# Attention weights kept as running products and met with differences of neighbouring values

## The chip, the cores and the metric

The kernel runs on one core of a Trainium2 chip. The core has five engines with instruction queues of their own, each worked off in order: TensorE (PE, matmuls and transposes; its weight loads are listed as PEld), VectorE (DVE), ScalarE (ACT), GpSimd (POOL) and SyncE (SP, which issues most DMAs here). The metric is the device time of one execution in microseconds (us).

## The reference

One decoder layer on 1,024 tokens and 16 meta tokens, width 1,024, all in float32. An input projection feeds four branches (a gated recurrence, a pooling branch, stick-breaking attention, a short convolution); they are gated, mixed and projected, and a squared-ReLU MLP follows. The change touches the attention branch alone, 8 heads of 64:

```python
def stick_breaking_attention(q, k, v, valid):
    # A[t,s] = sigmoid(z_ts) * prod_{s<j<t} (1 - sigmoid(z_tj)), s < t
    def one_block(args):                      # 128 queries
        ...
        z = jnp.einsum('bqhd,bkhd->bhqk', q_blk, kh) * scale
        log_keep = jnp.where(mask, jax.nn.log_sigmoid(-z), 0.0)
        between = lax.cumsum(log_keep, axis=3, reverse=True) - log_keep
        A = jnp.where(mask, jnp.exp(jax.nn.log_sigmoid(z) + between), 0.0)
        return jnp.einsum('bhqk,bkhd->bqhd', A, vh)
```

## The kernel before

The kernel is written in Python loops that are unrolled; a scheduler then puts each engine's instructions in an order of its own, with the order of the program as priority. What an engine runs is therefore not quite what the code's order says.

Every float32 product is done as two or three matmuls on a high part and a low part (`split`: ACT writes the high part, DVE subtracts it to get the low part). Tokens lie in reverse order of time, so that "earlier" keys have higher columns, and the 16 meta tokens come last, as a ninth block. `L` is 1,040, `P` is 128, `NB` is 8.

The attention works on pairs of heads (`Pair`, four of them): one pair's Q, K and V are 128 rows, 64 a head. A `Step` is one head `e` of the pair and one block `j` of 128 queries, with `n = 1040 - 128 j` keys (1,040, 912, ... 144): 16 steps to a pair, 64 in all. Each step has these parts:

- `scores`: PE makes the scores in chunks of up to 512 columns into the two banks `z`; ACT turns each chunk into `keep` (sigmoid of -z, shifted by a column) and `sig` (sigmoid of z); POOL masks the first 128 columns of both (`affine_select`); DVE forms the running product of `keep` with a scan, and multiplies `sig` by it. The result in `sig` are the attention weights.
- `turn`: PE transposes the weights, 128 columns at a time, into the two banks `tr`; `split` writes them to `at_h` and `at_l`.
- `combine`, once for two steps: PE multiplies `at_h` and `at_l` with the pair's values `vv` into the bank `av`; ACT copies one half to `fold`, DVE adds it to the other half into `br`, the branch's output.
- `values`, once for a pair: PE transposes the pair's V, and `vv` gets its high and low part.

Step i's scores are issued together with step i-1's transposes and, on odd i, with the `combine` of the two steps before. Between these parts stands filler: `fill` yields groups of three projection matmuls (the next pair's Q, K and V, 24 x 3,104 columns; for the last pair the first tile of the convolution branch), and after each part the loop takes up to `FILL` = 1,400 columns of it:

```python
for p in parts:
    if next(p, None) and i < NS:
        owed = spend(owed + FILL)
```

A pair has 65 parts that take filler, and 65 x 1,400 is more than 74,496 columns, so the filler of a pair ends before the pair does. Before the attention stand the norm of the tokens and the first pair's projections, behind it the recurrence, the pooling, the gates, the mixing and the MLP.

Of the kernel before, what the change touches and what calls it, by code (L numbers as in the profile page):

```python
# [10 lines left out]
F32 = mybir.dt.float32  # L11
# [4 lines left out]
ALU = mybir.AluOpType  # L16
# [15 lines left out]
WINDOWS = (2, 4, 8, 16)  # L32
FILL = 1400
QCH = [(0, 512), (512, 512)]
# [10 lines left out]
def hybrid_trunk_kernel(ctx: ExitStack, tc: tile.TileContext, x_tok, metas, vecs, gains, w_in, w_br, w_pool,  # L45
# [156 lines left out]
    with ExitStack() as st:  # L202
        pl = pool("attn", 1, None, st)
        VW = (NB + 1) * P
        sig = [new(pl, [P, VW], F32, f"sig{i}") for i in range(2)]
        keep = [new(pl, [P, (L, LP - 16)[i]], F32, f"keep{i}") for i in range(2)]
        for i in range(2):
            nc.gpsimd.memset(sig[i], 0.0)
            nc.gpsimd.memset(keep[i][:, 0:1], 1.0)
        A, B = slice(0, 64), slice(64, 128)  # L210
# [43 lines left out]
        class Pair:  # L254
            def __init__(self, pr):
                self.pr = pr
                self.qs, self.kh = ([new(pl, [P, w], F32R, tag, 4) for _ in range(2)]
                                    for w, tag in ((T, "qs"), (LP, "kh")))
                self.kl = kls[pr % 2 * 2:pr % 2 * 2 + 2]
                self.vt = new(loc, [P, L], F32, "a")  # L260

# [12 lines left out]

            def put_v(self, c0, n, ps):
                nc.scalar.copy(self.vt[:, c0:c0 + n], ps)

# [4 lines left out]

            def values(self):
                self.vv = vvs
                self.br = new(loc, [P, L], F32, "b")[:, :T]
                for b0 in range(0, NB + 1, 4):
                    nb = min(4, NB + 1 - b0)
                    rows = P if b0 < NB else NM
                    ps = bank("tr").rearrange("p (b c) -> p b c", c=P)[:rows, :nb]
                    for b in range(nb):  # L290
                        c0 = (b0 + b) * P
                        nc.tensor.transpose(ps[:, b, :], self.vt[:, c0:c0 + rows], ident)
                    for vv, (own, oth) in zip(self.vv, sides):
# [5 lines left out]
        class Step:  # L299
# [5 lines left out]
            def scores(self, i):  # L305
                n, e, j, pair = self.n, self.e, self.j, self.pair
                cw = n if n <= 512 else -(-n // (64 * -(-n // 512))) * 64
                sg, kp = self.sg, _ = sig[i % 2], keep[i % 2]
                lhs = pair.qs[e][:, j * P:(j + 1) * P]
                for c0 in range(0, n, cw):  # L310
# [4 lines left out]
                    nc.tensor.matmul(z, lhs, pair.kl[e][:, ks], start=False, stop=True)  # L315
                    w1 = min(w, n - 1 - c0)
                    nc.scalar.activation(kp[:, c0 + 1:c0 + 1 + w1], z[:, :w1], AF.Sigmoid, scale=-0.125)  # L317
                    nc.scalar.activation(sg[:, c0:c0 + w], z, AF.Sigmoid, scale=0.125)
                    if c0 + w < n:
                        yield True  # L320
                for t, fill in ((kp[:, 1:P + 1], 1.0), (sg[:, :P], 0.0)):
                    nc.gpsimd.affine_select(out=t, in_=t, compare_op=ALU.is_gt, fill=fill, base=0,  # L322
                                            pattern=[[1, P]], channel_multiplier=-1)
                nc.vector.tensor_tensor_scan(kp[:, 1:n], kp[:, 1:n], kp[:, 1:n], 1.0, op0=ALU.mult, op1=ALU.min)  # L324
                nc.vector.tensor_mul(sg[:, :n], sg[:, :n], kp[:, :n])  # L325
                yield True

            def turn(self, at):
                j, jj = self.j, self.j % 2
                per = -(-(NB + 1 - j) // -(-(NB + 1 - j) // 4))  # L330
                for b0 in range(0, NB + 1 - j, per):
                    nb = min(per, NB + 1 - j - b0)
                    ps = bank("tr").rearrange("p (b c) -> p b c", c=P)[:, :nb]
                    for b in range(nb):
                        nc.tensor.transpose(ps[:, b, :], self.sg[:, (b0 + b) * P:(b0 + b + 1) * P], ident)  # L335
                    dst = (slice(None), slice(j + b0, j + b0 + nb), slice(jj * P, (jj + 1) * P))
# [3 lines left out]
            def combine(self, at):  # L340
# [10 lines left out]
                nc.scalar.copy(fold[own], av[oth])  # L351
                nc.vector.tensor_add(pair.br[own, g * 2 * P:(g + 1) * 2 * P], av[own], fold[own])
                if e == 1 and g == NB // 2 - 1:
                    nc.sync.dma_start(br_dram[2, pair.pr], pair.br)
# [45 lines left out]
        NS = SBH * NB  # L400

        def spend(cols):
            while cols > 0:
                c = next(fill, None)
                if c is None:
                    return 0
                cols -= c
            return cols

        for i in range(NS + 2):  # L410
            parts, z, r = [], iter(()), i % (2 * NB)
            if i < NS:
                if r == 0:
                    spend(1 << 30)
                    pair = pairs[-1]
                    steps += [Step(pair, e, j) for e in range(2) for j in range(NB)]
                    if i + 2 * NB < NS:
# [4 lines left out]
                z = steps[i].scores(i)  # L422
                parts.append(z)
            if i % 2:
                if i > 1:
                    parts.append(steps[i - 2].combine(at))
                if r == 1 and i < NS:
                    parts.append(pair.values())
            if 1 <= i <= NS:
                if i % 2:  # L430
                    fresh = [new(pl, [P, NB + 1, 2 * P], F32R, n) for n in ("at_h", "at_l")]
                turn = steps[i - 1].turn(fresh)
                parts += [turn, z, turn, z, turn]
                at = fresh
            parts += [z, z]
            for p in parts:
                if next(p, None) and i < NS:
                    owed = spend(owed + FILL)
        spend(1 << 30)
# [782 lines left out]
```

## Time and profile before

| | us |
|---|---|
| median of 3 runs | 2023.66 (2022.07 to 2024.14) |
| the profiled execution | 2023.62 |
| its span in the profile | 2021.5 |
| PE busy in the span | 1950.3 |
| DVE busy | 1349.3 |
| ACT busy | 862.9 |
| POOL busy | 370.5 |

The span is what the profile covers from the first instruction to the last; 2.1 us lie around it. A busy time is the union of an engine's instruction spans. A matmul's span runs until its end, and the next one starts before that, so PE's rows overlap. In rows of the timeline the first column is the start in us from the span's start, the second the duration in us; in rows of groups the numbers after the bar are the busy time in us, the mean of one in ns, and the engine's idle time before them with what ended it. In the table of windows stand, after the window, its length and for each engine its busy time and number of instructions, then the granted TensorE clock, the DMA share and GB/s.

### The profile page before, as it was taken

Reading aid. Unit: us, or ns where it says so; the run is one execution under the profiler, and the core shown is the slowest. Engines: PE = TensorE matmul, PEld = TensorE weight load, DVE = VectorE, ACT = ScalarE, POOL = GpSimd, SP = SyncE. Lnnn points to the kernel's source line nnn. Section 1 sums busy time; section 2 is a strip of 40 time slices with the busy share of each in tenths; the row PEclk is TensorE's granted clock in tenths of the full one; section 3 lists DMA queues with packets and bytes.
Section 4 is the critical chain, followed back from the end, with each engine's and each line's share of the span. In section 5 each row is a group of like instructions: output and inputs, shape, how many; then the busy total and the mean of one; then the engine's idle time right before and its main releaser. Section 6 shows DMA issues by size and latency. Waiting matters only on the chain.

```text
span 2021.5 us, 25961 instructions
## 1 busy us (share of the span) xinstructions
PE 1950.3 (96%) x10006; PEld 1658.9 (82%) x10006; DVE 1349.3 (67%) x1784; ACT 862.9 (43%) x1478; POOL 370.5 (18%) x342
## 2 busy tenths in 40 slices
PE   9989889999999999999999999999999999999998
PEld 8778788888889997888887888887788888777876
DVE  6777887668777865334334567479555555878887
ACT  6566665333332323344333122254445554343435
POOL 1121222200010003323320000002232222322322
PEclk9999999999999999999999999999999999999999
DMA  3010110201101212232235555242545547344433
GB/s 137 32 32 22 32 32 22 69 22 43 53 22 53 89 63 94 104 125 105 104 125 200 211 182 172 72 142 83 145 131 157 164 149 257 131 137 138 162 126 137
DMA packets 109773, 216.23 MB, mean 107 GB/s; under 512 B 7873, under 2 KB 58561, under 8 KB 109650
## 3 DMA queue, kind: packets, MB, share of 16 engines
q1 hardware_dynamic: 55554, 171.02, 25.1%
q10 hardware_dynamic: 54096, 43.56, 6.5%
q8 instruction: 78, 1.28, 0.2%
q14 instruction: 45, 0.37, 0.1%
HBM read 153.21 MB, written 61.34 MB: 106 GB/s over the span
## 4 chain that ended last, share of the span: by engine, by line
PE 70%; DVE 14%; issue 7%; ACT 3%; DMA 3%; POOL 2%; DVEq 0%; POOLq 0%; ACTq 0%; SPq 0%
PE mm L702 16%; PE mm L100 10%; PE mm L99 10%; PE mm L101 10%; PE z L702 8%; PE tr L702 4%; PE mm L1070 3%; DVE keep L324 2%; PE z L564 1%; PE z L1070 1%; DVE wb L75 1%; DMA raw<-in_w_dn_dram 1%; DMA s_raw<-sum_dram 1%; PE av L348 1%; PE tr L335 1%
## 5 line engine op out<-in xcount | busy, mean ns | idle before, releaser
L99 PE MATMUL mm<-h_hi,hi 128*128 128x384 f32 (+4 forms) x1008 | 350.1, 348 | 0.4 <-ACT h_hi L74 0.3
L100 PE MATMUL mm<-h_lo,hi 128*128 128x384 f32 (+4 forms) x1008 | 346.0, 343 | 0.0
L101 PE MATMUL mm<-h_hi,lo 128*128 128x384 f32 (+4 forms) x1008 | 345.5, 343 | 0.0
L101 PEld LDWEIGHTS mm<-h_hi,lo 128*128 128x128 f32 x1008 | 190.3, 189 | 12.3
L100 PEld LDWEIGHTS mm<-h_lo,hi 128*128 128x128 f32 x1008 | 190.6, 189 | 11.7 <-DVE h_lo L75 0.6
L99 PEld LDWEIGHTS mm<-h_hi,hi 128*128 128x128 f32 x1008 | 190.0, 189 | 11.8 <-ACT h_hi L74 0.8
L679 POOL TENSOR_TENSOR sf<-raw 128x512 f32<-128x512 f32 x30 | 42.1, 1404 | 766.4 <-DMA raw<-in_w_up_dram 431.1
L75 DVE TENSOR_TENSOR sl<-sf,sh 128x1024 fp32r<-128x1024 f32 x60 | 74.4, 1242 | 106.5 <-ACT sh L74 106.5
L75 DVE TENSOR_TENSOR lo<-raw,hi 128x1024 fp32r<-128x1024 f32 x80 | 99.6, 1244 | 56.9 <-ACT hi L74 47.0
L74 ACT CAST hi<-raw 128x1024 fp32r<-128x1024 f32 x80 | 84.0, 1051 | 93.3 <-PE mm L100 58.2
L702 PE MATMUL mm<-th,sh 128*128 128x512 f32 x240 | 94.3, 393 | 8.8 <-ACT cc L707 8.8
L100 PE MATMUL mm<-b_lo,eh 128*128 128x512 f32 x256 | 100.1, 391 | 0.1
L101 PE MATMUL mm<-b_hi,el 128*128 128x512 f32 x256 | 99.6, 390 | 0.5 <-DVE el L75 0.5
L99 PE MATMUL mm<-b_hi,eh 128*128 128x512 f32 x256 | 99.6, 390 | 0.4 <-DVE mixed L862 0.4
L324 DVE TENSOR_TENSOR_SCAN keep<-keep 128x1039 f32<-128x1039 f32 (+3 forms) x64 | 89.0, 1394 | 7.9 <-ACT keep L317 4.4
L702 PE MATMUL mm<-tl,sh 128*128 128x512 f32 x240 | 93.9, 391 | 0.0
L702 PE MATMUL mm<-th,sl 128*128 128x512 f32 x240 | 93.9, 391 | 0.0
L74 ACT CAST sh<-sf 128x1024 fp32r<-128x1024 f32 x60 | 63.1, 1052 | 71.7 <-PE z L702 34.0
L322 POOL TENSOR_SCALAR_AFFINE_SELECT keep<-keep 128x128 f32<-128x128 f32 x64 | 35.0, 548 | 279.0 <-ACT keep L317 247.7
L75 DVE TENSOR_TENSOR el<-raw,eh 128x512 fp32r<-128x512 f32 x30 | 34.7, 1157 | 66.2 <-ACT eh L74 63.3
L75 DVE TENSOR_TENSOR at_l<-tr,at_h 128x384 fp32r<-128x384 f32 (+2 forms) x112 | 62.6, 567 | 22.5 <-ACT at_h L74 20.1
L335 PE MATMUL tr<-ident,sig 128*128 128x128 f32 x352 | 56.7, 276 | 20.6 <-DVE sig L325 14.4
(433 smaller groups left out, 4969.0 us busy)
## 6 DMA issues: line engine op xcount, KB each, us to landing
raw<-in_w_in_dram SPq DMA_DIRECT2D x76, 512.0 KB, 3.6
s_raw<-sum_dram SPq DMA_DIRECT2D x28, 896.0 KB, 4.8
gate_dram<-go ACTq DMA_DIRECT2D x32, 512.0 KB, 2.6
go<-gate_dram SPq DMA_DIRECT2D x32, 512.0 KB, 3.5
raw<-in_w_up_dram SPq DMA_DIRECT2D x32, 512.0 KB, 4.0
raw<-in_w_dn_dram SPq DMA_DIRECT2D x29, 512.0 KB, 4.3
sum_dram<-go ACTq DMA_DIRECT2D x52, 256.0 KB, 4.7
sum_dram<-sums ACTq DMA_DIRECT2D x39, 256.0 KB, 4.8
```

Of the source, the lines that this page charges most:

```text
L74: nc.scalar.copy(hi, src)
L75: (eng or nc.vector).tensor_sub(lo, src, hi.bitcast(F32))
L99: nc.tensor.matmul(ps, lh, rh, start=first, stop=False)
L100: nc.tensor.matmul(ps, lh, rl, start=False, stop=False)
L101: nc.tensor.matmul(ps, ll, rh, start=False, stop=last)
L322: nc.gpsimd.affine_select(out=t, in_=t, compare_op=ALU.is_gt, fill=fill, base=0, pattern=[[1, P]], channel_multiplier=-1)
L324: nc.vector.tensor_tensor_scan(kp[:, 1:n], kp[:, 1:n], kp[:, 1:n], 1.0, op0=ALU.mult, op1=ALU.min)
L335: nc.tensor.transpose(ps[:, b, :], self.sg[:, (b0 + b) * P:(b0 + b + 1) * P], ident)
L348: nc.tensor.matmul(av[:, :w], pair.vv[e][:, b, :], a[:, b, :w], start=i == 0 and a is at[0], stop=i == len(order) - 1 and a is at[1])
L679: nc.gpsimd.tensor_add(s12[:, 0], a21, a22)
L702: nc.tensor.matmul(ps, lhs[i][x][:, k, :], rhs[i][y][:, k, :], start=fresh and k == 0 and n == 0, stop=k == 3 and n == 2, skip_group_check ...
L1070: nc.tensor.matmul(ps, x, y[:, rs], start=fresh and k == 0 and n == 0, stop=k == 1 and n == 2, skip_group_check=not fresh)
```

## The change

With K as the running product, column 0 of it 1, the weight of a key is the difference of two neighbouring columns of K. So the sum over keys of weight times value is the same as the sum over columns of K times the difference of neighbouring values, plus what stands at the ends. The changed kernel leaves K as it is, and takes the differences of V once for a pair:

- `sig`, its sigmoid, its mask and its product with `keep` are gone. `turn` transposes `keep` (n + 1 columns matter, in as many blocks as before). There are three `keep` buffers of 1,152 columns, cleared by POOL at the start, where there were two each of `keep` and `sig`.
- `values` forms `step`: a subtraction on DVE of 1,039 columns, two copies of one column on ACT, and transposes `step` in place of V. A query block does not start at key 0, so the value just before it is added in `combine`: ACT copies those 8 columns to `edge`, and the one `tensor_add` of 256 columns becomes two `scalar_tensor_tensor` of 128.
- The select is issued behind the first chunk's sigmoid, not behind the last chunk's.
- The blocks of a head go in the order 0, 1, 6, 7, 2, 3, 4, 5.
- Filler is handed out in proportion to a step's keys: a step's share of 76,800 columns goes by n + 250, spread over its parts. `values` moves from round 1 to the end of round 2 of a pair, and the V tile is taken when V's first chunk is ready.

```diff
-FILL = 1400
+FILL = 1.0
+BLOCKS = (0, 1, 6, 7, 2, 3, 4, 5)
+FILL_COLS = 24 * (2 * LP + T)
...
-        sig = [new(pl, [P, VW], F32, f"sig{i}") for i in range(2)]
-        keep = [new(pl, [P, (L, LP - 16)[i]], F32, f"keep{i}") for i in range(2)]
...
+        keep = [new(pl, [P, VW], F32, f"keep{i}") for i in range(3)]
+        step = new(pl, [P, LP], F32, "step")
+        for t in keep:
+            nc.gpsimd.memset(t[:, 1:], 0.0)
+            nc.gpsimd.memset(t[:, :1], 1.0)
...
             def values(self):
                 self.vv = vvs
+                vt = self.vt
+                self.edge = new(pl, [P, 32], F32, "edge", 2)[:, :NB]
+                nc.scalar.copy(self.edge, vt[:, :T].rearrange("p (b k) -> p b k", k=P)[:, :, P - 1])
+                nc.scalar.copy(step[:, :1], vt[:, :1])
+                nc.scalar.mul(step[:, L:L + 1], vt[:, L - 1:L], -1.0)
+                nc.vector.tensor_sub(step[:, 1:L], vt[:, 1:L], vt[:, :L - 1])
...
-                    w1 = min(w, n - 1 - c0)
-                    nc.scalar.activation(kp[:, c0 + 1:c0 + 1 + w1], z[:, :w1], AF.Sigmoid, scale=-0.125)
-                    nc.scalar.activation(sg[:, c0:c0 + w], z, AF.Sigmoid, scale=0.125)
+                    t = kp[:, c0 + 1:c0 + 1 + w]
+                    nc.scalar.activation(t, z, AF.Sigmoid, scale=-0.125)
+                    if c0 == 0:
+                        nc.gpsimd.affine_select(out=t[:, :P], in_=t[:, :P], compare_op=ALU.is_gt, fill=1.0, base=0,
+                                                pattern=[[1, P]], channel_multiplier=-1)
...
-                for t, fill in ((kp[:, 1:P + 1], 1.0), (sg[:, :P], 0.0)):
-                    nc.gpsimd.affine_select(out=t, in_=t, compare_op=ALU.is_gt, fill=fill, base=0,
-                                            pattern=[[1, P]], channel_multiplier=-1)
-                nc.vector.tensor_tensor_scan(kp[:, 1:n], kp[:, 1:n], kp[:, 1:n], 1.0, op0=ALU.mult, op1=ALU.min)
-                nc.vector.tensor_mul(sg[:, :n], sg[:, :n], kp[:, :n])
+                t = kp[:, 1:n + 1]
+                nc.vector.tensor_tensor_scan(t, t, t, 1.0, op0=ALU.mult, op1=ALU.min)
...
-                nc.vector.tensor_add(pair.br[own, g * 2 * P:(g + 1) * 2 * P], av[own], fold[own])
+                for j in (2 * g, 2 * g + 1):
+                    js = slice(j % 2 * P, (j % 2 + 1) * P)
+                    nc.vector.scalar_tensor_tensor(pair.br[own, j * P:(j + 1) * P], av[own, js],
+                                                   pair.edge[own, j - 1:j] if j else 0.0, fold[own, js], op0=ALU.add,
+                                                   op1=ALU.add)
...
+        def quota(n):
+            return FILL * FILL_COLS * (n + 250) / (2 * sum(L - j * P + 250 for j in range(NB)))
...
-                    steps += [Step(pair, e, j) for e in range(2) for j in range(NB)]
+                    steps += [Step(pair, e, j) for e in range(2) for j in BLOCKS]
...
-                if next(p, None) and i < NS:
-                    owed = spend(owed + FILL)
+                if next(p, None) and i < NS:
+                    owed = spend(owed + quota(steps[i].n) / len(parts))
```

How the instructions stand shows at two places, both in the third pair. The first is on DVE, at the step of 656 keys of the pair's first head. `keep` is the running product, `at_l` the low part of transposed weights, `qs` the next pair's queries, `b` the branch's output. Before:

```order
L75 TENSOR_TENSOR at_l_2521<-tr_2559,at_h_2520 128x4x128
L324 SCALAR_TENSOR_TENSOR keep_14_106<-keep_14_106 128x655
L266 TENSOR_TENSOR qs_2334<-mm_2459,qs_2334 64x512
L325 TENSOR_TENSOR sig_12_104<-sig_12_104,keep_14_106 128x656
L75 TENSOR_TENSOR at_l_2521<-tr_2590,at_h_2520 128x3x128
L324 SCALAR_TENSOR_TENSOR keep_13_105<-keep_13_105 128x527
```

(The scan stands there as a scalar_tensor_tensor.) After:

```order
L77 TENSOR_TENSOR at_l_2410<-tr_2476,at_h_2409 128x2x128
L335 SCALAR_TENSOR_TENSOR keep_12_104<-keep_12_104 128x656
L268 TENSOR_TENSOR qs_2235<-mm_2338,qs_2235 64x512
L364 SCALAR_TENSOR_TENSOR b_2381<-av_2511,edge_2376,fold_2518 64x128 x2
L77 TENSOR_TENSOR at_l_2492<-tr_2525,at_h_2491 128x4x128
L77 TENSOR_TENSOR at_l_2492<-tr_2535,at_h_2491 128x3x128
L335 SCALAR_TENSOR_TENSOR keep_13_105<-keep_13_105 128x528
```

The product behind the scan is gone, so the transposes of this step wait for the scan alone, and other DVE work stands between two scans.

The second is on PE, towards the end of the third pair's second head, at the step of 528 keys. `mm` is filler, `z` scores, `tr` transposes, `av` the product with the values. Before:

```order
L99 MATMUL mm_2992<-h_hi_93,hi_2820 128x272
L100 MATMUL mm_2992<-h_lo_94,hi_2820 128x272
L101 MATMUL mm_2992<-h_hi_93,lo_2821 128x272
L335 MATMUL tr_3047<-ident_75,sig_12_104 128x128 x3
L314 MATMUL z_3053<-kh_1506,qs_1504 128x208
L315 MATMUL z_3053<-kl_16_112,qs_1504 128x208
L335 MATMUL tr_3064<-ident_75,sig_12_104 128x128 x3
L314 MATMUL z_3072<-kh_1506,qs_1504 128x400
L315 MATMUL z_3072<-kl_16_112,qs_1504 128x400
L348 MATMUL av_3083<-at_h_2959,vv_20_116 128x256
```

After:

```order
L325 MATMUL z_2944<-kh_1454,qs_1452 128x208
L326 MATMUL z_2944<-kl_16_114,qs_1452 128x208
L101 MATMUL mm_2927<-h_hi_93,hi_2742 128x272
L102 MATMUL mm_2927<-h_lo_94,hi_2742 128x272
L103 MATMUL mm_2927<-h_hi_93,lo_2743 128x272
L345 MATMUL tr_2952<-ident_75,keep_11_103 128x128 x3
L101 MATMUL mm_2927<-h_hi_93,hi_2742 128x272
L102 MATMUL mm_2927<-h_lo_94,hi_2742 128x272
L103 MATMUL mm_2927<-h_hi_93,lo_2743 128x272
L345 MATMUL tr_2961<-ident_75,keep_11_103 128x128 x3
```

Filler used to be at its end here; now three projection matmuls stand between the scores and each group of transposes, and six more follow before the next scores.

More of the change, by code (lines that the diff above doesn't have):

```diff
@@ L259, in __init__ @@
                 self.kl = kls[pr % 2 * 2:pr % 2 * 2 + 2]
-                self.vt = new(loc, [P, L], F32, "a")
+                self.vt = None
             def put_q(self, c0, n, ps):
@@ L275, in put_v @@
             def put_v(self, c0, n, ps):
+                if self.vt is None:
+                    self.vt = new(loc, [P, L], F32, "a")
                 nc.scalar.copy(self.vt[:, c0:c0 + n], ps)
@@ L287, in values @@
                     nb = min(4, NB + 1 - b0)
-                    rows = P if b0 < NB else NM
+                    rows = P if b0 < NB else NM + 1
                     ps = bank("tr").rearrange("p (b c) -> p b c", c=P)[:rows, :nb]
@@ L291, in values @@
                         c0 = (b0 + b) * P
-                        nc.tensor.transpose(ps[:, b, :], self.vt[:, c0:c0 + rows], ident)
+                        nc.tensor.transpose(ps[:, b, :], step[:, c0:c0 + rows], ident)
                     for vv, (own, oth) in zip(self.vv, sides):
@@ L307, in scores @@
                 cw = n if n <= 512 else -(-n // (64 * -(-n // 512))) * 64
-                sg, kp = self.sg, _ = sig[i % 2], keep[i % 2]
+                kp = self.kp = keep[i % 3]
                 lhs = pair.qs[e][:, j * P:(j + 1) * P]
@@ L334, in turn @@
                     for b in range(nb):
-                        nc.tensor.transpose(ps[:, b, :], self.sg[:, (b0 + b) * P:(b0 + b + 1) * P], ident)
+                        nc.tensor.transpose(ps[:, b, :], self.kp[:, (b0 + b) * P:(b0 + b + 1) * P], ident)
                     dst = (slice(None), slice(j + b0, j + b0 + nb), slice(jj * P, (jj + 1) * P))
@@ L351, in combine @@
                 nc.scalar.copy(fold[own], av[oth])
-                nc.vector.tensor_add(pair.br[own, g * 2 * P:(g + 1) * 2 * P], av[own], fold[own])
-                if e == 1 and g == NB // 2 - 1:
+                for j in (2 * g, 2 * g + 1):
[3 more added lines that the diff above has]
+                                                   op1=ALU.add)
+                if e == 1 and self.j == BLOCKS[-1]:
                     nc.sync.dma_start(br_dram[2, pair.pr], pair.br)
@@ L422, in hybrid_trunk_kernel @@
                 z = steps[i].scores(i)
-                parts.append(z)
+                parts += [z] * -(-steps[i].n // 512)
             if i % 2:
@@ L426, in hybrid_trunk_kernel @@
                     parts.append(steps[i - 2].combine(at))
-                if r == 1 and i < NS:
-                    parts.append(pair.values())
             if 1 <= i <= NS:
@@ L432, in hybrid_trunk_kernel @@
                 turn = steps[i - 1].turn(fresh)
-                parts += [turn, z, turn, z, turn]
+                parts += [turn] * -(-(NB + 1 - steps[i - 1].j) // 4)
                 at = fresh
-            parts += [z, z]
+            if r == 2 and i < NS:
+                parts.append(pair.values())
             for p in parts:
                 if next(p, None) and i < NS:
-                    owed = spend(owed + FILL)
+                    owed = spend(owed + quota(steps[i].n) / len(parts))
+            for p in parts:
+                assert next(p, None) is None
         spend(1 << 30)
```

3 lines of the change are left out of this document (removed).

## The prediction

> **What bounds the kernel now.** I read the page first, then a table of windows cut where the pairs begin, then the groups and waits of one pair, then the timeline around one stall. The page's busy totals and three of its slices (40 slices of some 50 us each):
>
> ```profile
> PE 1950.3 (96%) x10006; PEld 1658.9 (82%) x10006; DVE 1349.3 (67%) x1784; ACT 862.9 (43%) x1478; POOL 370.5 (18%) x342
> ...
> PE   9989889999999999999999999999999999999998
> PEld 8778788888889997888887888887788888777876
> DVE  6777887668777865334334567479555555878887
> ```
>
> PE is the bound over the whole kernel, and what it loses it loses in the first seven slices or so, where DVE is at 6 to 8 tenths. The windows: one row a pair of heads, then the start of the recurrence.
>
> ```profile
> 58.00:134.00 76.00, 67.17 (x414) 60.01 (x413) 58.13 (x75) 49.05 (x112) 13.73 (x30) 0.98 0.07 22
> 134.00:211.00 77.00, 69.91 (x451) 62.13 (x449) 63.45 (x90) 51.35 (x123) 14.63 (x32) 1.00 0.11 34
> 211.00:287.00 76.00, 68.66 (x444) 61.77 (x445) 62.75 (x89) 50.64 (x122) 15.56 (x33) 1.00 0.10 29
> 287.00:368.00 81.00, 73.29 (x476) 65.40 (x476) 65.41 (x94) 45.04 (x109) 19.81 (x36) 1.00 0.10 33
> 368.00:400.00 32.00, 32.00 (x183) 29.51 (x182) 18.70 (x33) 11.94 (x21) 6.92 (x5) 1.00 0.18 59
> ```
>
> The attention takes 310 us (58 to 368). In the steady third pair PE shows 68.66 of 76 us busy and DVE 62.75 (83%); behind the attention PE is full. But PE's rows overlap, so its true need comes from the distance between starts of unhindered neighbours:
>
> ```profile
> 336.15 0.39 PE L101 MATMUL mm<-h_hi,lo 128*128 128x512 f32 x1
> 336.38 0.40 PE L99 MATMUL mm<-h_hi,hi 128*128 128x512 f32 x1
> ...
> 242.34 0.31 PEld L335 LDWEIGHTS tr<-ident,sig 128*128 128x128 f32 x3 [1.78 <-issue]
> ```
>
> 512 columns last 0.39 us but the next matmul starts 0.23 us later: 0.449 ns a column. Three transposes load in 0.31 us: 0.105 us each. By the code a pair has 74,496 columns of filler, 18,944 of scores (two passes over 4,736 keys for two heads) and 22,528 against the values: 115,968 x 0.449 ns = 52.1 us. With 88 + 9 transposes at 0.105 (10.2 us) PE needs **62.3 us a pair**, and takes 76. So 13.7 us a pair are lost, 55 us in four: no change of DVE, ACT or POOL alone can give more.
>
> The Trainium skill, Perfetto Trace Analysis, section Identifying the Most-Contended Engine, says that the busy share of matmuls does not tell how close PE is to its limit, and sends the reader to the weight loads' busy share. Here the two differ as it says: 68.66 against 61.77 in the third pair; read by the first, only 29 us (7.3 x 4) could be won.
>
> Where the 13.7 us go, by waits in the third pair (engine and line that waits, what it waits for, us, times, longest):
>
> ```profile
> PEld tr L335 <- issue: 4.6, 3, 1.8
> PE tr L335 <- DVE sig L325: 3.7, 3, 1.5
> PEld z L314 <- ACT sig L318: 2.2, 4, 0.9
> PE tr L292 <- DVE vv L296: 1.5, 1, 1.5
> ```
>
> and one such stall in the timeline:
>
> ```profile
> 239.11 1.51 DVE L324 TENSOR_TENSOR_SCAN keep<-keep 128x655 f32<-128x655 f32 x1
> ...
> 239.67 1.04 POOL L322 TENSOR_SCALAR_AFFINE_SELECT keep<-keep 128x128 f32<-128x128 f32 x1 [6.07 <-ACT keep L317]
> ...
> 240.54 0.34 PE L101 MATMUL mm<-h_hi,lo 128*128 128x384 f32 x1
> 240.66 0.69 DVE L266 TENSOR_TENSOR qs<-mm,qs 64x512 fp32r<-64x512 f32 x1
> 240.67 0.29 POOL L322 TENSOR_SCALAR_AFFINE_SELECT sig<-sig 128x128 f32<-128x128 f32 x1
> 241.38 0.84 DVE L325 TENSOR_TENSOR sig<-sig,keep 128x656 f32<-128x656 f32 x1
> ...
> 242.37 0.52 PE L335 MATMUL tr<-ident,sig 128*128 128x128 f32 x3 [1.48 <-DVE sig L325]
> ```
>
> PE issues its last filler at 240.54, is through 0.17 us later, and stands until 242.37 because DVE, in order, does scan, `qs` and product before the transposes may start. That is the place the change works on: DVE is the engine that PE waits for, by the length of its queue and of the step's chain.
>
> **The change part by part.** DVE's and ACT's groups of the third pair:
>
> ```profile
> L324 DVE TENSOR_TENSOR_SCAN keep<-keep 128x271 f32<-128x271 f32 (+7 forms) x16 | 22.1, 1387 | 1.6 <-POOL keep L322 0.7 <-ACT keep L317 0.5
> L75 DVE TENSOR_TENSOR at_l<-tr,at_h 128x384 fp32r<-128x384 f32 (+2 forms) x29 | 16.1, 566 | 5.0 <-ACT at_h L74 4.9
> L325 DVE TENSOR_TENSOR sig<-sig,keep 128x272 f32<-128x272 f32 (+7 forms) x16 | 12.3, 776 | 0.9
> L352 DVE TENSOR_TENSOR b<-av,fold 64x256 f32<-64x256 f32 x9 | 3.8, 422 | 3.4 <-ACT fold L351 3.2
> ...
> L318 ACT ACTIVATE sig<-z 128x272 f32<-128x272 f32 (+8 forms) x29 | 13.1, 455 | 1.1 <-PE tr L335 1.1
> L317 ACT ACTIVATE keep<-z 128x384 f32<-128x384 f32 (+8 forms) x29 | 13.0, 452 | 6.5 <-PE z L315 4.3 <-DVE sig L325 2.1
> ```
>
> and the nearest rows for what is new:
>
> ```profile
> L325 DVE TENSOR_TENSOR sig<-sig,keep 128x1040 f32<-128x1040 f32 x8 | 10.2, 1273 | 0.6
> L325 DVE TENSOR_TENSOR sig<-sig,keep 128x144 f32<-128x144 f32 x8 | 2.4, 301 | 0.4
> ...
> 223.53 0.20 ACT L295 CAST vv<-tr 16x64 fp32r<-16x64 f32 x1
> ...
> 224.18 0.21 DVE L296 TENSOR_TENSOR vv<-tr,vv 16x64 fp32r<-16x64 f32 x1
> ```
>
> On DVE: The product goes: 16 x 0.776 = -12.4 us a pair. The difference of V is one product-like operation on 1,039 columns: +1.27, once. Eight additions of 256 columns (0.422, 3.4 us) become sixteen of 128: at least 0.21 each (the row of 64 columns), at most 0.42 (no faster than twice as wide), so 0.0 to +3.4; I take 0.29, just under the 0.301 of 144 columns: +1.3. The scan runs over one column more: nothing at 1,387 ns. Net -9.8 us (-11.1 to -7.7): DVE from 62.8 to 53.0 us a pair, under PE's 62.3.
>
> On ACT: The second sigmoid goes, -13.1 us; three small copies come, 0.20 to 0.31 each, +0.6 to 0.9. ACT falls from 50.6 to about 38, nowhere near a bound. What counts is that a bank `z` is free after one sigmoid and not two (0.46 us sooner): the 2.2 us of score loads waiting for `sig` mostly go.
>
> On PE: The same columns and transposes. `values` transposes 17 rows where it had 16: nothing.
>
> On POOL: One select a step goes. At the start POOL clears three buffers where it cleared two (a buffer is 1.06 us in the row below) ahead of `kl`:
>
> ```profile
> 2.31 1.06 POOL L208 MEMSET sig<- 128x1152 f32 x1
> ...
> 3.46 4.14 POOL L217 MEMSET kl<- 64x1088 f32 x4
> ...
> 18.06 0.35 ACT L271 CAST kh<-mm 64x256 fp32r<-64x256 f32 x1
> ```
>
> `kl` is done near 8.7 us in place of 7.6; keys are first written at 18.06, so this costs nothing; without that cover it would be 1.1 us.
>
> What is moved: SP's DMAs are the same and in the same order. The order of blocks and the filler's shares change what PE has to do between a step's last score and its first transpose. Counting rows of PE's order in the third pair at the prices above, this cover was 2.5 us (656 keys, second head) to 6.0, mostly 4 to 5; it becomes 4.4 to 7.4. The chain that it has to cover is a sigmoid (0.45), the scan and what stands before it in DVE's queue; the product's 0.78 (1.27 at 1,040 keys) is no longer in it. `values` goes to the end of round 2, where the step of 272 keys keeps DVE least busy; its wait (1.5 us for `vv`) stays in part, since the first `combine` needs `vv` soon after.
>
> The sum: Nothing here is on the path by itself; it all shows in PE's 13.7 lost us a pair. From below, only waits that name the product go: 3.7 us, 15 in all. From above all of it: 55. DVE gives up 9.8 a pair, and if DVE alone set the pace that would be 39. Taking PE's need as the new floor, something stays: the `vv` wait (1 us), waits of `combine` for the last `at_l` (some 0.5), tr banks held while a scan of up to 2.3 us stands before their `at_l` (two long scans come next to each other at each head's start, 1 to 2 us), and the small gaps. I put that at 5.7 of the 13.7, so 8.0 us a pair are won: 32 us, nearer DVE's 39 than the 15. The profiled execution took 2023.6 (span 2021.5 and 2.1 around it), within 0.1 of the median: 2023.6 - 32 = **1991.6 us**.
>
> **The rivals.**
>
> First, the new order holds DVE to local peaks. The long steps, `step`, `vv` and `qs` come together at a pair's start; there DVE has about as much to do as PE. Then only the named waits and part of the rest go, 3.7 to 5 us a pair: 2023.6 - 17 = 2006. For it: DVE would still be 85% busy of PE's need (53.0 of 62.3), as it is 83% now. Against: the filler is now heaviest in the long steps, so PE has work there.
>
> Second, PE reaches its floor. All but some 2 us a pair go: -47 us, 1977. For it: covers over 4.4 us everywhere, DVE with 9 us to spare. Against: even now, with covers of 5, small gaps exist.
>
> Third, and slower: selects stand in the way of the scans. A select now stands behind the first chunk's sigmoid, so it meets the scan of the step before; POOL's groups:
>
> ```profile
> L322 POOL TENSOR_SCALAR_AFFINE_SELECT keep<-keep 128x128 f32<-128x128 f32 x16 | 9.9, 616 | 56.7 <-ACT keep L317 47.4 <-PE tr L335 6.5 <-PE mm L101 2.8
> L322 POOL TENSOR_SCALAR_AFFINE_SELECT sig<-sig 128x128 f32<-128x128 f32 x17 | 6.1, 361 | 4.5 <-ACT sig L318 4.0
> ```
>
> The select at 239.67 lasted 1.04 us, until 0.09 after the scan of 239.11 ended; the one at 240.67, beside another DVE operation, 0.29. If each of 64 steps' scans waited 1.04 us for its select, that is 66 us against the 32 won: 2023.6 - 32 + 66 = 2058. It decides from 0.5 us a step on. Against: a held select ends with the scan before it, and `at_l` work stands between two scans; DVE's wait for a select is 0.7 us a pair now. The Trainium skill, SBUF — State Buffer, section Who interferes with whom, says that a DVE instruction with two inputs in SBUF and a GpSimd instruction that reads SBUF exclude each other, whichever is second waiting until the first is through; the trace agrees (1.04 us, above).
>
> Fourth, no change to speak of. The waits move behind other DVE work (`at_l`, `qs`) of the same queue. Against: DVE's total falls by 9.8 us a pair.
>
> **How the numbers follow.** Forecast 0.60 (1981 to 2001, from 5.7 to 10.7 us a pair), local peaks 0.19, PE's floor 0.13, slower 0.04, no change 0.04. The range that leaves out no more than 2 in 10 takes the forecast, most of the floor and most of the peaks: 1977 to 2009 (15 us won, the named waits alone). A measurement of this kernel tells about 0.2% (4 us) from no change; faster by more 0.92, within 0.04, slower 0.04.
>
> **What would show it.** Right: the four windows of a pair near 68 us, the attention some 32 us shorter, every later stage as long as before; DVE near 53 us and ACT near 38 a pair; one sigmoid, one select and one scan a step, no product; PE's waits for the scan short, none over 1.5 us but at a pair's start. The forecast's size is wrong if DVE's split additions cost 0.42 each, if PE's transposes still wait about 4 us a pair for the scans, or if the scans wait for selects. It is wrong in kind if the time lost in the attention stays near 55 us while DVE's busy time falls.

## The result, and the profile after

The changed kernel takes 1993.09 us (median of four runs, 1989.07 to 1993.61), the kernel before, timed beside it, 2023.90 (2022.07 to 2025.92): a ratio of 0.9843, 95% interval 0.9826 to 0.9860. The profiled execution took 1993.61 us (span 1991.4), the one of before 2023.62 (span 2021.5): 30.0 us less. The forecast was 32 us less, 1991.6.

Where the time went shows at the last product with the values, the end of the attention. From the timeline of PE, before and then after:

```profile
369.36 0.28 PE L348 MATMUL av<-at_l,vv 128*128 128x256 f32 x1
```

```profile
338.87 0.28 PE L358 MATMUL av<-at_l,vv 128*128 128x256 f32 x1
```

The attention ends 30.5 us sooner. From there to the end of the span it is 2021.5 - 369.4 = 1652.1 us before and 1991.4 - 338.9 = 1652.5 after: no later stage changed. Since the runs of the kernel before differ between comparisons (medians of 2020.4 to 2023.9), this end of the attention in the profile is used below as the finer measure. It is taken from one execution of each kernel.

Not all of the 30.5 us is the change's work. In the profile of before, right behind PE's longest wait, the granted clock is about half for 3.3 us, and matmuls of 384 columns start 0.32 us apart (109.29 and 109.61) where they start 0.18 apart a little later (112.31 and 112.49). The wait in the timeline, then the window behind it:

```profile
107.95 0.58 PE L335 MATMUL tr<-ident,sig 128*128 128x128 f32 x3 [1.84 <-DVE sig L325]
```

```profile
108.20:111.50 3.30, 3.30 (x13) 3.30 (x12) 2.41 (x4) 1.57 (x4) 0.00 (x0) 0.51 0.35 57
```

That is 3.3 x 0.49 = 1.6 us lost to the clock, so some 29 us are left for the change. The attention of after and of the runs below shows a clock of 1.00. Whether the wait brought the clock down no run shows; behind two waits of 1.5 us, at 166.86 and 188.58, the clock stayed at 1.00.

The table of windows of after, one row a pair, cut where the pairs begin (length, then busy time and count of PE, PEld, DVE, ACT and POOL, clock, DMA share, GB/s), and the same of before in one row for the whole attention, then of after:

```profile
58.50:127.40 68.90, 66.03 (x429) 59.51 (x427) 51.46 (x75) 43.31 (x95) 5.67 (x16) 1.00 0.08 24
127.40:196.70 69.30, 67.07 (x443) 61.35 (x442) 53.42 (x81) 41.57 (x96) 5.15 (x16) 1.00 0.10 31
196.70:266.10 69.40, 67.16 (x445) 61.41 (x443) 53.50 (x81) 41.63 (x96) 5.15 (x16) 1.00 0.09 31
266.10:338.90 72.80, 70.86 (x474) 65.30 (x472) 56.11 (x84) 35.16 (x80) 10.63 (x19) 1.00 0.13 44
```

```profile
58.70:369.40 310.70, 279.73 (x1786) 249.78 (x1785) 250.46 (x346) 196.10 (x465) 65.14 (x131) 0.99 0.09 30
```

```profile
58.50:338.90 280.40, 271.11 (x1781) 247.57 (x1780) 214.49 (x318) 161.67 (x364) 26.61 (x67) 1.00 0.10 33
```

PE's weight loads are as long as before (249.8 and 247.6 us) in a tenth less time. DVE gave up 36.0 us, ACT 34.4, POOL 38.5. In the third pair, whose rows the prediction used, DVE fell from 62.75 to 53.50 us.

What PE waits for over the whole attention (engine and line that waits, what it waits for, us, times, longest), the largest rows of before and then of after:

```profile
PEld tr L335 <- issue: 17.5, 14, 2.1
PE tr L335 <- DVE sig L325: 14.4, 13, 1.8
PEld av L348 <- DVE at_l L75: 9.9, 21, 1.3
...
PEld z L314 <- ACT sig L318: 4.4, 11, 0.9
PE tr L292 <- DVE vv L296: 4.0, 3, 1.6
```

```profile
PEld tr L345 <- DVE at_l L77: 7.0, 14, 0.9
PEld av L358 <- DVE at_l L77: 5.8, 11, 1.2
PE tr L345 <- DVE at_l L77: 3.3, 5, 0.9
...
PEld tr L345 <- DVE keep L335: 0.7, 1, 0.7
PEld z L325 <- ACT keep L328: 0.6, 2, 0.3
...
PEld tr L345 <- issue: 0.2, 1, 0.2
```

The 14.4 us behind the product are gone, and nothing like them stands behind the scan (0.7 us in one wait). The largest row of before, the 17.5 us of `issue` (a wait for which the profile shows no cause), goes with them: it is the same stalls, seen at the weight load. In the stall that the prediction shows, the load at 242.34 has 1.78 us of `issue` and its matmul at 242.37 has 1.48 behind the product; so it is with eight of the 14 waits, 13.5 of the 17.5 us. The two rows must not be added. What is left are waits for `at_l`: for a bank `tr` to come free, and for the low part of the weights ahead of the product with the values.

### The profile page after: what moved, and what is told of

It reads as the page before. It is cut to its first block, busy times and chain, and to the rows that moved or that the text cites. A ratio compares the mean times of both kernels' runs of the same rounds, so it can differ in the third digit from the quotient of the medians.

```text
span 1991.4 us, 25654 instructions
## 1 busy us (share of the span) xinstructions
PE 1941.8 (98%) x10006; PEld 1657.5 (83%) x10006; DVE 1314.9 (66%) x1756; ACT 828.1 (42%) x1378; POOL 331.9 (17%) x280
## 4 chain that ended last, share of the span: by engine, by line
PE 73%; DVE 12%; issue 8%; DMA 3%; ACT 3%; POOL 1%; POOLq 0%; DVEq 0%; SPq 0%; ACTq 0%
PE mm L720 16%; PE mm L102 10%; PE mm L101 10%; PE mm L103 10%; PE z L720 8%; PE tr L720 4%; PE mm L1088 3%; PE av L358 2%; PE z L1088 2%; PE z L582 1%; DMA s_raw<-sum_dram 1%; PE tr L1088 1%; DVE keep L335 1%; PE tr L345 1%; DVE wa L77 1%
## 5 line engine op out<-in xcount | busy, mean ns | idle before, releaser
L335 DVE TENSOR_TENSOR_SCAN keep<-keep 128x1040 f32<-128x1040 f32 (+3 forms) x64 | 89.0, 1390 | 24.6 <-ACT keep L328 18.2
L330 POOL TENSOR_SCALAR_AFFINE_SELECT keep<-keep 128x128 f32<-128x128 f32 x64 | 23.9, 373 | 300.6 <-ACT keep L328 262.2
L76 ACT CAST at_h<-tr 128x384 fp32r<-128x384 f32 (+2 forms) x112 | 54.3, 495 | 40.8 <-PE tr L345 36.9
L76 ACT CAST s_hi<-s_raw 128x1280 fp32r<-128x1280 f32 x28 | 35.4, 1266 | 82.9 <-DMA s_raw<-sum_dram 76.3
```

What stands on the lines that cost most here:

```text
L76: nc.scalar.copy(hi, src)
L330: nc.gpsimd.affine_select(out=t[:, :P], in_=t[:, :P], compare_op=ALU.is_gt, fill=1.0, base=0, pattern=[[1, P]], channel_multiplier=-1)
L335: nc.vector.tensor_tensor_scan(t, t, t, 1.0, op0=ALU.mult, op1=ALU.min)
```

## The experiments

The prediction had said that PE waits for DVE "by the length of its queue and of the step's chain". These are two things. The first four runs ask which of them it is, and how much of the gain is the arithmetic's and how much the order's; "attention" is the end of the attention in the profile. Each ratio is to the kernel before as it was timed beside that run, with medians of 2020.4 to 2021.3 for e1 to e12 and 2023.90 for the changed kernel. So runs are compared with each other by their medians and by the attention: e7 is as fast as the changed kernel in both and has 0.9871.

| run | median us | ratio to before (95%) | attention, us |
|---|---|---|---|
| before | 2023.90 | 1 | 369.4 |
| after | 1993.09 | 0.9843 (0.9826 to 0.9860) | 338.9 |
| e1 arithmetic alone | 2003.07 | 0.9907 (0.9892 to 0.9922) | 349.0 |
| e2 order alone | 2018.40 | 0.9985 (0.9975 to 0.9995) | 362.1 |
| e3 more DVE work, off the chain | 1996.47 | 0.9876 (0.9859 to 0.9894) | 343.5 |
| e4 more DVE work, on the chain | 2016.80 | 0.9974 (0.9964 to 0.9985) | 362.2 |
| e5 second sigmoid | 2003.05 | 0.9916 (0.9902 to 0.9929) | 349.1 |
| e6 even filler | 2002.59 | 0.9912 (0.9899 to 0.9926) | 349.1 |
| e7 select last | 1993.36 | 0.9871 (0.9856 to 0.9886) | 338.5 |
| e8 old parts | 2014.16 | 0.9965 (0.9956 to 0.9974) | see below |
| e9 old parts, full shares | 2002.95 | 0.9901 (0.9882 to 0.9920) | 348.9 |
| e10 scan by chunk | 1990.11 | 0.9840 (0.9823 to 0.9857) | 335.5 |
| e11 blocks in a row | 1994.88 | 0.9865 (0.9849 to 0.9882) | 340.3 |
| e12 by chunk, filler by n + 400 | 1989.90 | 0.9845 (0.9832 to 0.9859) | 335.2 |

**Arithmetic alone, order alone.** e1 is the changed kernel with everything that orders work put back; e2 is the changed kernel with `sig`, its sigmoid, its mask and its product put back and the values as before, so that only the order is new.

```diff
 e1, against the changed kernel
-BLOCKS = (0, 1, 6, 7, 2, 3, 4, 5)
+BLOCKS = tuple(range(NB))
 # select behind the last chunk; parts as before; values in round 1
-                    owed = spend(owed + quota(steps[i].n) / len(parts))
+                    owed = spend(owed + 1400)
```

> Running products and value differences as in the changed kernel, but everything of the order as before: blocks 0 to 7, 1,400 columns of filler a part, the parts in the old sequence, values in round 1, the select behind the last chunk. If the shorter DVE queue and chain are the cause (mine), most of the 30 us stay: 1996 to 2004 us. If the order of blocks and filler is the cause (rival), at most a third stays: 2013 us or more.

> The kernel before with sig, its sigmoid and its product, but with the new order: blocks 0, 1, 6, 7, 2, 3, 4, 5, filler in proportion to the keys, the new sequence of parts, values at the end of round 2, both selects behind the first chunk. If DVE's work is the cause (mine), DVE keeps 62.8 us a pair beside PE's 62.3 and the time is 2010 to 2020 us. If the order is the cause (rival), 2003 us or less.

Both came within what was expected. The arithmetic alone shortens the attention by 20.4 us, the order alone by 7.3; both together by 30.5, so the order is worth 10 once the product is gone. The 1.6 us of low clock in before are in the first three of these figures, and by the medians beside their own before it is 18.2 and 2.9 us; e2's profiled execution was its fastest (2015.08). The arithmetic alone does not take the waits behind the scan away, as the rows of e1 show:

```profile
PEld tr L344 <- issue: 12.0, 17, 1.7
PE tr L344 <- DVE keep L334: 4.1, 7, 1.3
```

**The same DVE work in two places.** Both add one multiplication by one over a step's keys, as long as the removed product, to every step: 62 of 766 ns in e3, which starts with the third step, and 64 of 781 ns in e4, about 50 us. In e4 it stands behind the step's own scan, so the transposes wait for it; in e3 it works on the `keep` of two steps ago, for which nobody waits but the next scores in that buffer (ACT three times, 4.8 us in all). The scheduler also gave e3's a place of its own: at the third pair's start those of 528 and 400 columns ran at 202.25 and 205.10, ahead of the scans at 202.86 and 206.16 that they follow in the program. `one` is a column of ones, made at the start.

```diff
 e4
                 nc.vector.tensor_tensor_scan(t, t, t, 1.0, op0=ALU.mult, op1=ALU.min)
+                nc.vector.tensor_mul(t, t, one.broadcast_to([P, n]))
 e3
                 nc.vector.tensor_tensor_scan(t, t, t, 1.0, op0=ALU.mult, op1=ALU.min)
+                if i > 1:
+                    m = steps[i - 2].n
+                    u = keep[(i - 2) % 3][:, 1:m + 1]
+                    nc.vector.tensor_mul(u, u, one.broadcast_to([P, m]))
```

> The changed kernel, and on DVE in each step one more multiplication by one of the running product of two steps ago, in place, after its transposes have read it: DVE's queue gets back some 12 us a pair, the chain of the step stays short. If the length of DVE's queue is what PE waits for (mine), 2005 to 2015 us. If the chain's latency is what counts (rival), under 1999 us.

> The changed kernel with the running product multiplied by one, in place, behind the scan and ahead of the transposes: the same DVE work as in the run before it, but now in the step's chain. If the queue is what counts (mine), within 4 us of the run with the work off the chain: 2006 to 2018 us. If the chain's latency is what counts (rival), 8 us or more above that run.

The table of windows over the attention, of e3 and then of e4:

```profile
58.10:343.50 285.40, 273.51 (x1785) 248.51 (x1784) 253.37 (x380) 161.10 (x364) 32.03 (x67) 1.00 0.10 32
```

```profile
58.10:362.20 304.10, 275.63 (x1785) 248.78 (x1784) 260.16 (x382) 161.64 (x364) 31.96 (x67) 1.00 0.09 30
```

In e3 DVE is busy for 253.4 of 285.4 us (89%, more than the 81% of before), and the attention is 4.6 us longer than after. In e4 it is 260.2 of 304.1 (86%), and it is 23.3 us longer: more than the whole gain of the arithmetic, 20.4, is gone. It ends where e2 ends (362.2 and 362.1), which has the product itself and also the second sigmoid and select: one DVE operation in the product's place undoes all that the arithmetic brings in this order. By time e3 stands 8 us under what the theory of the queue gave, and e4 20 us above e3. So how full DVE is hardly counts; what stands ahead of the DVE result that PE needs next does. The groups of DVE over the attention, first e3, then e4, show where the room was:

```profile
L337 DVE TENSOR_TENSOR_SCAN keep<-keep 128x1040 f32<-128x1040 f32 (+3 forms) x64 | 88.7, 1385 | 6.6 <-ACT keep L330 5.6 <-POOL keep L332 0.4 <-issue 0.3
L77 DVE TENSOR_TENSOR at_l<-tr,at_h 128x384 fp32r<-128x384 f32 (+2 forms) x112 | 62.2, 567 | 3.1 <-ACT at_h L76 2.1
L341 DVE TENSOR_TENSOR keep<-keep,one 128x1040 f32<-128x1040 f32 (+7 forms) x62 | 47.5, 766 | 6.2 <-PE tr L351 6.0
```

```profile
L338 DVE TENSOR_TENSOR keep<-keep,one 128x1040 f32<-128x1040 f32 (+3 forms) x64 | 50.0, 781 | 1.6
```

and in after, from 58.5 to 338.9:

```profile
L335 DVE TENSOR_TENSOR_SCAN keep<-keep 128x1040 f32<-128x1040 f32 (+3 forms) x64 | 89.0, 1390 | 24.6 <-ACT keep L328 18.2 <-POOL keep L330 6.1
L77 DVE TENSOR_TENSOR at_l<-tr,at_h 128x384 fp32r<-128x384 f32 (+2 forms) x112 | 61.7, 568 | 12.3 <-ACT at_h L76 10.9
L364 DVE SCALAR_TENSOR_TENSOR b<-av,edge,fold 64x128 f32<-64x128 f32 x54 | 16.8, 344 | 1.1 <-ACT fold L361 0.6
...
L364 DVE SCALAR_TENSOR_TENSOR b<-av,fold 64x128 f32<-64x128 f32 x8 | 2.3, 289 | 7.6 <-ACT fold L361 7.5
```

After has 36.9 us in which DVE stood idle before scans and `at_l`; in e3 9.7 of them are left, so more than half of its 47.5 us of multiplications went into that room. Where e4 loses its time shows in PE's waits, e3 first, then e4:

```profile
PE av L364 <- DVE at_l L77: 6.5, 11, 1.0
PE tr L351 <- DVE at_l L77: 3.1, 7, 0.5
```

```profile
PE tr L348 <- DVE at_l L77: 13.2, 16, 1.8
PE av L361 <- DVE at_l L77: 6.8, 11, 1.0
PE tr L348 <- DVE keep L338: 4.8, 4, 1.2
```

Ahead of the product with the values the two are alike (6.5 and 6.8 us). Ahead of the transposes PE waits 3.3 us in e3 (3.1, and 0.2 for the scan) and 18.0 in e4: 14.7 of the 18.7 us by which e4's attention is longer. The wait there ends last mostly with an `at_l` that frees a bank `tr` (13.2), less often with the multiplication itself (4.8). e4 does not separate these two ways in which its multiplication is in front: the transposes wait for it, and so does an `at_l` that is queued behind it.

**The same on ScalarE.** e5 lengthens the chain without touching DVE: each chunk's sigmoid is done twice.

```diff
+                    nc.scalar.activation(t, z, AF.Sigmoid, scale=0.125)
                     nc.scalar.activation(t, z, AF.Sigmoid, scale=-0.125)
```

> The changed kernel, with each chunk's sigmoid done twice on ScalarE into the same columns: 13 us a pair more on ScalarE, no more on VectorE, and each score bank held 0.45 us longer. Theory (what counts is the delay from a step's last score to its first transpose, on whatever engine): every step's chain grows by at least the 0.45 us of its last chunk, 29 us over 64 steps; at the price seen for work put on the chain on VectorE (23 us lost for 50 us of work, 0.47) that is 13 us: 2000 to 2012. Rival (the chain matters on VectorE alone, whose queue PE waits for; ScalarE has 27 us a pair to spare): 1990 to 1997. ScalarE busy some 51 us a pair in both.

The windows and the first waits of PE of e5:

```profile
58.20:349.10 290.90, 272.40 (x1780) 248.05 (x1779) 214.65 (x318) 207.13 (x476) 25.93 (x67) 1.00 0.10 32
```

```profile
PEld tr L346 <- DVE at_l L77: 10.2, 13, 1.3
PEld av L359 <- DVE at_l L77: 10.0, 15, 1.6
PE tr L346 <- DVE at_l L77: 7.1, 9, 1.0
```

DVE does what it did in after (214.65 us), ACT is busy for 71% of the time, and the attention is 10.2 us longer, inside what the delay of the chain foretold. PE's waits name DVE, which is not the one that has more to do: `at_l` is late because what comes before it is. The second sigmoid also stands ahead of `at_h` in ACT's queue, but by DVE's waits the delay comes through the scans. Two rows of what DVE waits for in e5:

```profile
DVE keep L336 <- ACT keep L329: 29.1, 32, 2.0
DVE at_l L77 <- ACT at_h L76: 8.2, 13, 1.6
```

In after the scans wait 18.2 us for sigmoids and `at_l` 10.9 for `at_h`: the first has grown, the second has not.

**Which part of the order.** Five runs put back one part of the order each in the changed kernel, e8 and e9 the same one.

```diff
 e6
-                    owed = spend(owed + quota(steps[i].n) / len(parts))
+                    owed = spend(owed + 1400)
 e7: affine_select of the first 128 columns behind the last chunk's sigmoid
 e8
-                parts += [z] * -(-steps[i].n // 512)
+                parts.append(z)
+                if r == 1 and i < NS:
+                    parts.append(pair.values())
-                parts += [turn] * -(-(NB + 1 - steps[i - 1].j) // 4)
+                parts += [turn, z, turn, z, turn]
-            if r == 2 and i < NS:
-                parts.append(pair.values())
+            parts += [z, z]
 e9: as e8, and
-                    owed = spend(owed + quota(steps[i].n) / len(parts))
+                    owed = spend(owed + quota(steps[i].n) / useful)
 e11
-BLOCKS = (0, 1, 6, 7, 2, 3, 4, 5)
+BLOCKS = tuple(range(NB))
```

In e9 `useful` counts the parts that have something to issue.

> The changed kernel, with up to 1,400 columns of filler after each part, as before, in place of shares by the number of keys; blocks, select and parts stay as changed. Theory (the gain of the new order, 10 us, comes from filler being there when a long chain has to be covered and lasting to the pair's end): most of the 10 us is lost, 1997 to 2005, and PE waits for the transposes of a pair's last steps. Rival (the gain comes from the order of the blocks or of the parts): 1990 to 1996.

> The changed kernel, with the select behind the sigmoid of the last chunk, where it stood before, and not behind the first. Theory (delay of the chain): in the 32 steps of more than 512 keys the select joins the chain, 0.3 us each, 10 us of chain at the price of 0.47: 4 to 5 us, so 1994 to 2000. Rival (a select behind the first chunk runs into the scan of the step before and is held): without it faster, 1986 to 1992.

> The changed kernel, with the sequence of a step's parts as before (scores, transposes, combine, with empty turns between, and the values in round 1 of a pair in place of the end of round 2); filler by the number of keys, blocks and select stay as changed. Theory (the shares of filler do it, the sequence little): 1991 to 1997. Rival (the sequence, or where the values stand, carries the order's 10 us): 1998 to 2006, with the loss at the pairs' starts.

> As the run before with the old sequence of parts (2014 us), but each step's share is divided by the parts that take filler and not by all: there, half of a pair's filler (36,480 of 74,496 columns, 109 matmuls in one piece) was left for the pair's end. Theory (the shares of filler do it, the sequence of parts little): 1991 to 1997. Rival (the sequence, or where the values stand, matters by itself): 2000 to 2010.

> The changed kernel, with the blocks of a head in the order 0 to 7, as before; shares, select and parts stay as changed. Theory (the shares of filler carry the order's gain): 1991 to 1998. Rival (blocks 6 and 7 behind 0 and 1, where the values are made, carry a good part): 1999 to 2006, with the loss at the starts of the heads.

e6 came where the theory had it: 2002.59, as slow as with the whole order undone (e1). The sign that the theory named did not show, though: in e6 PE waits for scans ahead of transposes for 1.2 us only (3 times). What grew are its waits for `at_l` ahead of the product with the values (7.5 us in 11 waits, 2.8 in 3 after) and for sigmoids to free a bank of scores (2.5 us, none after). And e9 is as slow, too, with 2002.95, and there the theory was wrong: the shares of filler alone do not do it. Either without the other is worth nothing that shows; together they bring the 10 us. e9 changes two things, the sequence of the parts and the place of `values`; which of them it is was not tried. The largest waits of PE in e9 stand at the transposes again, as in before:

```profile
PEld tr L345 <- issue: 16.1, 19, 1.4
PE tr L345 <- DVE at_l L77: 10.8, 13, 1.3
PE tr L345 <- DVE keep L335: 6.3, 8, 1.2
```

e8 was an edit that did something else than meant. A part that is through takes no filler, and the old sequence has many of these, so half of a pair's filler was left to the pair's end; the window of one such stretch:

```profile
118.80:133.80 15.00, 15.00 (x103) 15.00 (x102) 4.38 (x9) 6.12 (x14) 0.00 (x0) 1.00 0.14 37
```

Here PE has 15 us without a gap and DVE 4.4 us to do, and the first three pairs take 74 us each: filler that is not there while DVE works is worth nothing. (In the last pair what is left slips behind the attention, so its end says nothing for this run.)

The select's place makes no difference (1993.36; 338.5): it came between the two ranges, so a select behind the last chunk does not lengthen the chain by anything that is seen, and one behind the first is not in the way of the scan before. The row of waits in e7, 6.1 us in 15 waits as in after:

```profile
DVE keep L334 <- POOL keep L332: 6.1, 15, 0.9
```

The order of the blocks is worth some 1.4 us of the attention (e11).

**A version that goes further.** If the delay counts, a shorter chain should help. In e10 each chunk has its own scan, which starts from the last column of the chunk before; e12 also gives short steps more filler.

```diff
 e10
-                    if c0 + w < n:
-                        yield True
-                t = kp[:, 1:n + 1]
-                nc.vector.tensor_tensor_scan(t, t, t, 1.0, op0=ALU.mult, op1=ALU.min)
-                yield True
+                    nc.vector.tensor_tensor_scan(t, t, t, kp[:, c0:c0 + 1] if c0 else 1.0, op0=ALU.mult, op1=ALU.min)
+                    yield True
 e12: as e10, and n + 400 in quota in place of n + 250
```

> The changed kernel, with the running product taken chunk by chunk: a scan behind each chunk's sigmoid that starts from the last column of the one before, 12 scans a pair more. VectorE gets 12 x 0.2 us = 2.4 us a pair more to do; in 10 of a pair's 16 steps the last scan covers 208 to 400 columns and not 528 to 1,040, which takes 0.65 to 1.5 us out of the chain, some 10 us a pair. Theory (the delay of the chain is what PE waits for): a third to a half of the 6 us still lost a pair goes, 8 to 12 us in all: 1980 to 1988. Rival (VectorE's queue, or the other chains that are left, from the last low part of the weights to the product with the values): 1990 to 1998.

> The version with a scan for each chunk (1990 us), with filler by n + 400 in place of n + 250: the step of 144 keys gets a quarter more, the step of 1,040 a tenth less. Theory: with the long steps' chains cut short, what is still lost lies behind the short steps (0.6 to 0.8 us a pair where the transposes behind the scores of 144 keys wait for the low part before them, some 1 us around the making of the values); more filler there takes half of it: 1984 to 1989. Rival (the long steps need what they have: even filler cost 10 us): 1992 to 2000.

e10's attention is 3.4 us shorter than after's: less than half of the 8 to 12 that the theory asked, and its median lies in the rival's range (1990 to 1998), outside the theory's. e12's attention is 3.7 shorter, its median between its two ranges, so its filler adds nothing that can be told. The medians of 1990.1 and 1989.9 are the lowest of all, but neither was timed beside the changed kernel, and their ratios to before are the changed kernel's (0.9840 and 0.9845 to 0.9843); that they beat it is likely by the profiles and not shown by the times. What e10 took away is the wait for `at_l` ahead of the product with the values, 2.8 us in three waits, at the start of a second head. This is a chain that the rival had named. The timeline of after shows one, DVE and then PE:

```profile
236.77 2.33 DVE L335 TENSOR_TENSOR_SCAN keep<-keep 128x1040 f32<-128x1040 f32 x1
239.13 0.56 DVE L275 TENSOR_TENSOR kl<-mm,kh 64x384 fp32r<-64x384 f32 x1
239.72 0.69 DVE L77 TENSOR_TENSOR at_l<-tr,at_h 128x512 fp32r<-128x512 f32 x1
```

```profile
239.24 0.28 PE L358 MATMUL av<-at_h,vv 128*128 128x256 f32 x1
240.47 0.39 PE L358 MATMUL av<-at_l,vv 128*128 128x256 f32 x1 [0.95 <-DVE at_l L77]
```

The scan of 1,040 keys holds DVE for 2.33 us while `kl` and `at_l` are queued behind it, and PE stands until 240.47. In e10 that scan is in three pieces, of which the last takes 0.77 us, and PE runs through the same place:

```profile
234.75 0.77 DVE L332 TENSOR_TENSOR_SCAN keep<-keep 128x272 f32<-128x272 f32 x1
```

```profile
237.21 0.28 PE L355 MATMUL av<-at_h,vv 128*128 128x256 f32 x1
237.33 0.28 PE L355 MATMUL av<-at_l,vv 128*128 128x256 f32 x1
```

## Why the prediction was right, and where it was not

**The size.** Pairs of 75.6, 77.0, 75.5 and 82.6 us (from the first scores of one to those of the next, the last to the attention's end) became 68.9, 69.3, 69.4 and 72.8: 6.7, 7.7, 6.1 and 9.8 us, a mean of 7.6 where 8.0 were forecast. Of the 7.6, 0.4 are the low clock in the first pair of before. Against PE's need of 62.3 the first three pairs still lose 6.6 to 7.1 us, where the residue was put at 5.7. Of its terms, the one for `combine` was mis-sized: 0.5 us a pair for the last `at_l`, measured 5.8 us in four pairs by PE's weight loads, 1.4 a pair. The banks `tr` (7.0 in four, 1.75 a pair) are within the 1 to 2 given. The terms that the prediction names add up to 2.5 to 3.5 us; the rest of the 5.7 was left to small gaps, for which it shows no row. Its list of waits also counts stalls twice, some 3 us of the 12.0 in its four rows: two of the three `issue` waits have a matmul behind them that is listed as waiting for the product. The forecast does not use that sum.

**DVE's sum.** Product -12.4 as forecast (64 x 776 ns before), the difference of V 1.22 us where 1.27 was taken. The split additions took 344 ns with a column of `edge` and 289 ns with the constant 0, where 0.29 was assumed for all: 19.1 us of busy time for 62 in place of 13.1 for 31, some 1.6 a pair and not 1.3. By these rows DVE's net is -9.6, where -9.8 was forecast; the union of its spans fell by 9.0 a pair.

**ACT.** About 38 us a pair was forecast from the third pair's rows; 41.6 came there, and 40.4 as the mean of four (161.67 / 4). The union fell by 34.4 us in four pairs, less than the 112 sigmoids of 0.455 us add up to (51.0), though the busy times of ACT's groups, added up, fell by 50.2 (219.1 to 168.9): neighbouring rows of ACT overlap, so a mean of one times a count, taken from a union, takes off too much.

**The covers and small waits.** Waits of scores for a bank went from 4.4 to 0.6 us, as said. None of PE's waits in the attention is over 1.2 us. The selects did not get into the scans' way: the mean of `keep`'s select fell from 548 to 373 ns, and DVE waits for selects of `keep` 6.1 us in all (2.2 before), 0.10 a step, where that rival needed 0.5.

**The step that failed** is half of the reason, not the number: "by the length of its queue" in "DVE is the engine that PE waits for, by the length of its queue and of the step's chain", and with it the yardstick "nearer DVE's 39", as if the 9.8 us a pair that DVE gives up were what PE gets back. e3 gives DVE all of that back (253.37 against 214.49 us, 9.7 a pair) and costs 4.6 us in the whole attention; e4 gives back the same work where the product stood (260.16) and costs 23.3. How much DVE has to do was a small cause at most. The product cost what it did by its place, ahead of the transposes and of the `at_l` that frees their bank; which of these two holds PE is not shown. e5 shows that a delay on ACT ahead of the scan costs PE time, too. The Trainium skill, Perfetto Trace Analysis, section Optimization Strategies, says to optimize, when the matmul engine waits, the engines that block the critical path; e3 and e4 agree, and show that the engine's name is not enough for that (4.6 and 23.3 us on the same engine). That 8.0 a pair came out nearly right rests on the floor of PE's need, which holds whichever of the two reasons is true, and on a residue that was in part a guess.

**The order** was in the prediction as a longer cover (4.4 to 7.4 us) without a price of its own. It is a third of the gain, 10 of 30 us, and only as a whole: without it the result would have stood nearer to "local peaks" (2006) than to the forecast (1991.6), since e1, e6 and e9 all stand near 2003. A forecast that gave the order no price and met the sum of both was lucky in this.

## What to carry to other kernels

When PE waits for an engine that is 80% busy, ask for what stands ahead of the one result that it needs next, not how full the engine is: the same 50 us of DVE work cost 5 us in one place and 23 in another. Filler is worth what it covers: half of it left in one piece at a pair's end made a pair 74 us long where 69 were possible, and handing it out evenly cost 10 us in all. A wait names what is last in a chain, not what made the chain late. A long operation of an in-order engine delays everything queued behind it; cutting it in pieces may help those rather than its own chain.

## What the runs showed of the hardware that was not expected

A `scalar_tensor_tensor` of 64x128 with one input in PSUM took 344 ns with a per-partition scalar from SBUF and 289 ns with a constant. How much of the 55 ns is the scalar's alone is not shown: the eight with the constant stand behind idle time (7.6 us before them), most of the 54 others do not (1.1 us). A scan cut in pieces paid little for it; the group of e10 in the third pair:

```profile
L332 DVE TENSOR_TENSOR_SCAN keep<-keep 128x384 f32<-128x384 f32 (+8 forms) x28 | 24.8, 886 | 6.2 <-POOL keep L330 5.1
```

After takes 22.2 us for the 16 scans of a pair (1,390 ns each), so each of the 12 more costs 0.2 us.
